# Sum of squares at the head of a projection: seven tiles added on GpSimd, then two ones-products in place of eight

## The chip, the cores and the metric

The kernel runs on one core of a Trainium2 chip. A core has five engines that each take their own queue of instructions in order: TensorE (matrix products, PE in the rows, its weight loads PEld), VectorE (DVE), ScalarE (ACT), GpSimd (POOL) and SyncE (SP, which issues most DMAs). The metric is the device time of one execution in microseconds, and lower is better. Before the change it is 3444.31 us, the median of three runs (3441.16 to 3452.11).

## What is computed

Two blocks stand one behind the other. The first has two layers, each with two attention mixers and an MLP, on 512 tokens of 1024 features. The second has an MLA layer and a GLA layer, each with an MLP, on the same 512 latent tokens and on 256 context tokens. What matters here is the norm ahead of each projection:

```python
def rms_norm(x, g):
    xf = x.astype(jnp.float32)
    y = xf * lax.rsqrt(jnp.mean(xf * xf, axis=-1, keepdims=True) + RMS_EPS)
    return (y * g.astype(jnp.float32)).astype(x.dtype)
...
    x = x + rms_norm(mixed, norm_g[1])
    hf = rms_norm(x, norm_g[2])
    ff = jnp.square(jax.nn.relu(hf @ w_ff1)) @ w_ff2
    return x + rms_norm(ff, norm_g[3])
```

In the second block the norm's output is modulated: `h * (1 + scale) + shift`. So each projection's output goes through a norm, is added to the residual x, and x goes through the next norm, whose output feeds the next projection. All is float32.

## The kernel before

**Layout.** Activations lie feature-major: x is eight tiles (k = 0 to 7) of 128 features on the partitions by the tokens on the free axis. The latent stream L has 512 tokens in two slices `sl` of 256, the context stream C has one slice of 256. A norm's sum runs over features, thus over partitions and over the eight tiles. It is formed on TensorE: a product with a 128 x 128 matrix of ones (`total`, line 280) adds up the partitions and leaves the sum in all of them, in PSUM.

**Projections.** A float32 matrix product is done as three products of rounded operands (`mac3`, lines 211 to 213): an activation has a high and a low part (h, lo), a weight too (wh, wl). Weights come by DMA into a raw tile; ScalarE casts the high part (line 190) and GpSimd, in a few places VectorE, subtracts to get the low one (line 194). The split of weights is the bulk of GpSimd's work.

**The norm at the head.** `sum_sq` squares one tile on ScalarE (line 322) into a scratch tile, the slice of S.y that the residual has just used up or a temporary tile t where there is no y, and makes the product with ones at once, eight products that accumulate in one PSUM tile. `inv_rms` then makes the factor: a Ln on ScalarE (line 146) that reads the PSUM tile, VectorE's copy of the mean into S.acc (line 260), an Exp and three short VectorE steps of a Newton correction. There are two users. `prep_plain` (first block) makes the parts h and lo without the factor, so its matmuls wait for h and lo alone and the factor comes in behind them. `prep_mod` (second block) needs the factor first: sum of eight squares, factor, and then per tile one VectorE, one ScalarE and one VectorE step to h and lo.

**The residual ahead of it.** The steps over k come from `residual`, which makes the previous norm's factor r from S.acc (sum of squares that lines 291 to 299 added up beside the previous projection, some on GpSimd, the rest on VectorE, and one ones-product) and then does for each tile two VectorE instructions, lines 308 and 309:

```python
nc.vector.scalar_tensor_tensor(y, y, gs[:, k:k + 1], r, op0=ALU.mult, op1=ALU.mult)
nc.vector.tensor_tensor(x, x, y, op=ALU.add)
yield k
```

At each yield `sum_sq` squares the new x. Three norms have no residual in front: the two slices of the very first norm, and the context's first norm in the second block; their x comes by DMA. In all there are 19 norms of 256 tokens of this kind: 2 at the start (11 to 38 us), 2 at 493 to 520, 2 at 872 to 902, 2 at 1354 to 1381, the context's first at 1420 to 1447, 2 at 1741 to 1794, 3 at 2111 to 2164, 3 at 2668 to 2731 and 2 at 3040 to 3077.

**The order.** These norms are generators, which the projection in front advances between its groups of matmuls (`chain`, `tick`, `ready`, lines 112 to 132): the norm of slice 0 runs while TensorE still works on slice 1. Each engine's queue is laid out when the program is built, by a scheduler that has its own estimates of durations. On the chip every engine takes its queue strictly in order; an instruction that waits holds up what stands behind it.

Of the kernel before, what the change touches and what calls it, by code (L numbers as in the profile page):

```python
# [14 lines left out]
AF = mybir.ActivationFunctionType  # L15
ALU = mybir.AluOpType
# [6 lines left out]
KT = D // P  # L23
# [27 lines left out]
class Builder:  # L51
# [265 lines left out]
            return S.y[:, k, sl]  # L317
        return self.t(self.tmp, [P, 512], F32, tag="t")[:, :256]

    def sum_sq(self, S, k, sl, ps):  # L320
        q = self.scratch(S, k, sl)
        self.nc.scalar.activation(q, S.x[:, k, sl], AF.Square)
        return self.total(q, ps, k == 0, k == KT - 1)

    def prep_plain(self, S, sl, gs, steps):

        nc = self.nc
        ps = None
        for k in steps:
            h, lo = (p[:, sl] for p in S.ht[k])  # L330
            x, g = S.x[:, k, sl], gs[:, k:k + 1]
            nc.scalar.activation(h, x, AF.Copy, scale=g)  # L332
            nc.vector.scalar_tensor_tensor(lo, x, g, h.bitcast(F32), op0=ALU.mult, op1=ALU.subtract)
            ps = self.sum_sq(S, k, sl, ps)
            yield
        self.inv_rms(ps, D, S.r[:, sl], S.acc[:, sl])

    def prep_mod(self, S, sl, gs, sh, steps):

        nc = self.nc  # L340
        ps = None
        for k in steps:
            ps = self.sum_sq(S, k, sl, ps)
            yield
        r = self.t(self.rp, [P, 256], F32, tag="ry", bufs=6)
        self.inv_rms(ps, D, r, S.acc[:, sl])
        for k in range(KT):
            h, lo = (p[:, sl] for p in S.ht[k])
            t = self.scratch(S, k, sl)
            nc.vector.scalar_tensor_tensor(t, S.x[:, k, sl], gs[:, k:k + 1], r, op0=ALU.mult, op1=ALU.mult)  # L350
            nc.scalar.activation(h, t, AF.Identity, bias=sh[:, k:k + 1])
            nc.vector.scalar_tensor_tensor(lo, t, sh[:, k:k + 1], h.bitcast(F32), op0=ALU.add, op1=ALU.subtract)
            yield
# [1998 lines left out]
```

## Time and profile before

| | |
|---|---|
| time, median of 3 runs | 3444.31 us |
| the profiled execution | 3443.82 us |
| its span, first to last instruction | 3442.1 us |
| mean granted TensorE clock | 0.98 |
| TensorE busy | 3267.2 us, 95% |
| VectorE busy | 2147.2 us, 62% |
| ScalarE busy | 1512.3 us, 44% |
| GpSimd busy | 1174.1 us, 34% |

A row of the timeline has the start, the duration, engine, line, operation, the program's names out<-in, the shape, how many instructions the row merges, and in brackets the idle time of that engine just before, with what ended it. A row that merges several instructions spans from the first one's start to the last one's end, and rows of different lines can lie over each other in time. A float32 product shows as two rows of TensorE. In a window, the granted clock is the share of full speed (1.00 is 2.4 GHz, 0.50 is 1.2 GHz) that TensorE had, as a mean over the stretch. Numbers in brackets behind a busy time are counts of instructions.

### The profile page before, as it was taken

Reading aid. Unit: us, or ns where it says so; the run is one execution under the profiler, and the core shown is the slowest. Engines: PE = TensorE matmul, PEld = TensorE weight load, DVE = VectorE, ACT = ScalarE, POOL = GpSimd, SP = SyncE. Lnnn points to the kernel's source line nnn. Section 1 sums busy time; section 2 is a strip of 40 time slices with the busy share of each in tenths; the row PEclk is TensorE's granted clock in tenths of the full one; section 3 lists DMA queues with packets and bytes.
Section 4 is the critical chain, followed back from the end, with each engine's and each line's share of the span. In section 5 each row is a group of like instructions: output and inputs, shape, how many; then the busy total and the mean of one; then the engine's idle time right before and its main releaser. Section 6 shows DMA issues by size and latency. Waiting matters only on the chain.

```text
span 3442.1 us, 48999 instructions
## 1 busy us (share of the span) xinstructions
PE 3267.2 (95%) x18723; PEld 2826.3 (82%) x18723; DVE 2147.2 (62%) x4036; ACT 1512.3 (44%) x3323; POOL 1174.1 (34%) x688
## 2 busy tenths in 40 slices
PE   8899989999899998999999999999999899989998
PEld 8788778878878877778888878888888888878887
DVE  6855677875875567676577764333334767873445
ACT  5445544232545554422256664422222566653223
POOL 3333334444323333344422332222223222124443
PEclk8999999999999999999999999999999999999999
DMA  5212464553321245465321122122212221123332
GB/s 177 66 61 71 147 196 141 184 166 110 108 68 59 71 147 178 147 197 168 94 69 33 48 88 69 57 67 62 62 62 63 65 63 57 61 77 102 98 98 68
DMA packets 262098, 337.69 MB, mean 98 GB/s; under 512 B 17107, under 2 KB 178110, under 8 KB 261734
## 3 DMA queue, kind: packets, MB, share of 16 engines
q1 hardware_dynamic: 261862, 334.55, 31.0%
q8 instruction: 147, 2.41, 0.3%
q14 instruction: 89, 0.73, 0.1%
HBM read 305.98 MB, written 28.52 MB: 97 GB/s over the span
## 4 chain that ended last, share of the span: by engine, by line
PE 69%; DVE 16%; ACT 7%; issue 4%; DMA 2%; POOL 1%; SPq 0%; DVEq 0%; ACTq 0%; POOLq 0%
PE mm L211 15%; PE mm L213 15%; PE mm L212 15%; PE s L212 4%; PE s L211 4%; PE s L213 4%; PE s L280 2%; ACT wh L190 1%; DMA araw<-in_ada_w_dram 1%; POOL wl L194 1%; PE tp L1065 1%; PE mm L238 1%; PE mm L239 1%; PE mm L240 1%; DVE y L308 1%
## 5 line engine op out<-in xcount | busy, mean ns | idle before, releaser
L194 POOL TENSOR_TENSOR wl<-wraw,wh 128x1024 fp32r<-128x1024 f32 (+2 forms) x424 | 993.3, 2361 | 1750.8 <-ACT wh L190 1703.2
L211 PE MATMUL mm<-h,wh 128*128 128x512 f32 (+1 forms) x1916 | 723.2, 378 | 31.1 <-ACT h L332 9.5
L213 PE MATMUL mm<-h,wh 128*128 128x512 f32 (+1 forms) x1916 | 710.5, 372 | 3.6 <-DVE h L1265 1.6
L212 PE MATMUL mm<-h,wl 128*128 128x512 f32 (+1 forms) x1916 | 711.1, 371 | 0.5 <-DVE wl L194 0.4
L190 ACT CAST wh<-wraw 128x1024 fp32r<-128x1024 f32 (+3 forms) x454 | 428.7, 967 | 534.2 <-issue 366.6
L211 PEld LDWEIGHTS mm<-h,wh 128*128 128x128 f32 x1916 | 367.6, 192 | 94.8 <-ACT h L1264 10.7
L213 PEld LDWEIGHTS mm<-h,wh 128*128 128x128 f32 x1916 | 367.0, 192 | 67.7 <-DVE h L1265 4.8
L212 PEld LDWEIGHTS mm<-h,wl 128*128 128x128 f32 x1916 | 368.0, 192 | 51.9 <-POOL wl L194 0.8
L529 DVE TENSOR_TENSOR t<-t 128x512 f32<-128x512 f32 (+1 forms) x140 | 173.1, 1237 | 255.2 <-ACT hid L525 255.1
L211 PE MATMUL mm<-hid,wh 128*128 128x512 f32 (+1 forms) x848 | 292.5, 345 | 9.8 <-DVE y L541 9.7
L213 PE MATMUL mm<-hid,wh 128*128 128x512 f32 (+1 forms) x848 | 289.9, 342 | 0.0
L212 PE MATMUL mm<-hid,wl 128*128 128x512 f32 (+1 forms) x848 | 289.7, 342 | 0.0
L1381 DVE SCALAR_TENSOR_TENSOR tp<-araw,sc,tp 128x512 f32<-128x512 f32 x280 | 200.7, 751 | 57.6 <-DMA araw<-in_ada_w_dram 56.2
L541 DVE TENSOR_TENSOR y<-y,mm 128x512 f32<-128x512 f32 (+1 forms) x192 | 105.4, 549 | 196.4 <-PE mm L213 196.4
L530 DVE TENSOR_TENSOR hid<-t,hid 128x512 fp32r<-128x512 f32 (+1 forms) x176 | 199.5, 1138 | 29.0 <-ACT t L527 24.3
L213 PE MATMUL s<-hid,wh 128*128 128x512 f32 (+1 forms) x560 | 208.7, 373 | 0.0
L211 PE MATMUL s<-hid,wh 128*128 128x512 f32 (+1 forms) x560 | 208.6, 373 | 0.0
L212 PE MATMUL s<-hid,wl 128*128 128x512 f32 (+1 forms) x560 | 208.4, 372 | 0.0
L525 ACT ACTIVATE hid<-t 128x512 fp32r<-128x512 f32 (+1 forms) x176 | 97.4, 555 | 219.7 <-DVE t L522 144.0
L211 PEld LDWEIGHTS mm<-hid,wh 128*128 128x128 f32 x848 | 159.2, 188 | 34.1 <-DVE y L541 6.8
L213 PEld LDWEIGHTS mm<-hid,wh 128*128 128x128 f32 x848 | 159.2, 188 | 20.9
L212 PEld LDWEIGHTS mm<-hid,wl 128*128 128x128 f32 x848 | 159.2, 188 | 20.8
(683 smaller groups left out, 7362.5 us busy)
## 6 DMA issues: line engine op xcount, KB each, us to landing
wraw<-in_w_ff_dram SPq DMA_DIRECT2D x128, 512.0 KB
wraw<-in_mlp_w_dram SPq DMA_DIRECT2D x128, 512.0 KB
araw<-in_ada_w_dram SPq DMA_DIRECT2D x96, 512.0 KB
wraw<-in_w_in_dram SPq DMA_DIRECT2D x68, 512.0 KB
raw<-in_cmp_w_dram SPq DMA_DIRECT2D x16, 512.0 KB
td<-t SPq DMA_DIRECT2D x32, 256.0 KB
h<-td SPq DMA_DIRECT2D x32, 256.0 KB
wraw<-in_w_out_dram SPq DMA_DIRECT2D x16, 512.0 KB
```

The source lines that it names most:

```text
L190: i = nc.scalar.copy(h[:, x:z], raw[:, x - a:z - a]).ins
L194: e.tensor_tensor(l[:, x:z], raw[:, x - a:z - a], h[:, x:z].bitcast(F32), op=ALU.subtract)
L211: nc.tensor.matmul(ps, wh, mh, start=first, stop=False)
L212: nc.tensor.matmul(ps, wl, mh, start=False, stop=False)
L213: nc.tensor.matmul(ps, wh, ml, start=False, stop=last)
L238: nc.tensor.matmul(ps, h[:, sl], w[0][:, k, :n], start=k == 0, stop=False)
L280: self.nc.tensor.matmul(ps, self.ones, acc, start=first, stop=last)
L525: nc.scalar.activation(h, a, AF.Square)
L529: nc.vector.tensor_tensor(a, a, a, op=ALU.mult)
L530: nc.vector.tensor_tensor(lo, a, h.bitcast(F32), op=ALU.subtract)
L541: nc.vector.tensor_tensor(y, y, ps, op=ALU.add)
L1381: nc.vector.scalar_tensor_tensor(a, raw[:, k], sc, a, op0=ALU.mult, op1=ALU.add)
```

## The change

The square of tile 0 goes to S.acc directly. The squares of tiles 1 to 6 go to the scratch as before, and GpSimd adds each to S.acc (the new line 328). Tile 7's square isn't added: the sum over partitions is now two products, one of S.acc and one of tile 7's square, which accumulate in one PSUM tile. So each of the 19 norms has 2 products where it had 8, and 6 adds on GpSimd. S.acc is free then: the residual in front has read it last in its Newton step. The lines behind move by three.

```diff
--- before.py
+++ after.py
@@ -317,30 +317,33 @@
             return S.y[:, k, sl]
         return self.t(self.tmp, [P, 512], F32, tag="t")[:, :256]
 
-    def sum_sq(self, S, k, sl, ps):
-        q = self.scratch(S, k, sl)
-        self.nc.scalar.activation(q, S.x[:, k, sl], AF.Square)
-        return self.total(q, ps, k == 0, k == KT - 1)
+    def sum_sq(self, S, k, sl):
+
+        nc, acc = self.nc, S.acc[:, sl]
+        q = acc if k == 0 else self.scratch(S, k, sl)
+        nc.scalar.activation(q, S.x[:, k, sl], AF.Square)
+        if k == KT - 1:
+            return self.total(q, self.total(acc, None, True, False), False, True)
+        if k:
+            nc.gpsimd.tensor_tensor(acc, acc, q, op=ALU.add)
 
     def prep_plain(self, S, sl, gs, steps):
 
         nc = self.nc
-        ps = None
         for k in steps:
             h, lo = (p[:, sl] for p in S.ht[k])
             x, g = S.x[:, k, sl], gs[:, k:k + 1]
             nc.scalar.activation(h, x, AF.Copy, scale=g)
             nc.vector.scalar_tensor_tensor(lo, x, g, h.bitcast(F32), op0=ALU.mult, op1=ALU.subtract)
-            ps = self.sum_sq(S, k, sl, ps)
+            ps = self.sum_sq(S, k, sl)
             yield
         self.inv_rms(ps, D, S.r[:, sl], S.acc[:, sl])
 
     def prep_mod(self, S, sl, gs, sh, steps):
 
         nc = self.nc
-        ps = None
         for k in steps:
-            ps = self.sum_sq(S, k, sl, ps)
+            ps = self.sum_sq(S, k, sl)
             yield
         r = self.t(self.rp, [P, 256], F32, tag="ry", bufs=6)
         self.inv_rms(ps, D, r, S.acc[:, sl])
```

Of GpSimd's queue this is the place of the two norms at 493 to 520 us. Names: wl is a weight's low part (line 194), acc_95 is S.acc, t and y are squares. Before:

```order
L194 TENSOR_TENSOR wl_4909<-wraw_4910,wh_4908 128x1024
L194 TENSOR_TENSOR wl_4909<-wraw_4914,wh_4908 128x1024
L299 TENSOR_TENSOR acc_95<-acc_95,t_5060 128x256
L299 TENSOR_TENSOR acc_95<-acc_95,t_5089 128x256
L194 TENSOR_TENSOR wl_5223<-wraw_5224,wh_5222 128x512
L194 TENSOR_TENSOR wl_5223<-wraw_5230,wh_5222 128x512
L299 TENSOR_TENSOR acc_95<-acc_95,t_5141 128x256
L194 TENSOR_TENSOR wl_5249<-wraw_5250,wh_5248 128x512
L194 TENSOR_TENSOR wl_5249<-wraw_5256,wh_5248 128x512
L194 TENSOR_TENSOR wl_5618<-wraw_5619,wh_5617 128x1024
L194 TENSOR_TENSOR wl_5618<-wraw_5623,wh_5617 128x1024
L194 TENSOR_TENSOR wl_5712<-wraw_5713,wh_5711 128x1024
```

Now:

```order
L194 TENSOR_TENSOR wl_5219<-wraw_5220,wh_5218 128x512
L194 TENSOR_TENSOR wl_5219<-wraw_5226,wh_5218 128x512
L299 TENSOR_TENSOR acc_95<-acc_95,t_5137 128x256
L328 TENSOR_TENSOR acc_95<-acc_95,y_4752 128x256 x3
L194 TENSOR_TENSOR wl_5245<-wraw_5246,wh_5244 128x512
L328 TENSOR_TENSOR acc_95<-acc_95,y_4752 128x256 x2
L194 TENSOR_TENSOR wl_5245<-wraw_5252,wh_5244 128x512
L328 TENSOR_TENSOR acc_95<-acc_95,y_4752 128x256 x7
L194 TENSOR_TENSOR wl_5616<-wraw_5617,wh_5615 128x1024
L194 TENSOR_TENSOR wl_5616<-wraw_5621,wh_5615 128x1024
L194 TENSOR_TENSOR wl_5710<-wraw_5711,wh_5709 128x1024
```

The twelve adds of both slices stand among the weight splits, three ahead of the second pair's first split, two between its halves and seven behind.

Of TensorE's queue this is the norm of slice 1 at 2135 us. mm_21058 (now mm_21055) and s_21102 (now s_21099) are tiles of the MLP's first product on slice 0, which needs nothing of this norm; s_20955 (now s_21008) is the norm's sum. Before:

```order
L213 MATMUL mm_21058<-h_20197,wh_21030 128x256
L280 MATMUL s_20955<-y_3748_20259,ones_89 128x256
L211 MATMUL mm_21058<-h_20202,wh_21030 128x256
L212 MATMUL mm_21058<-h_20202,wl_21031 128x256
L213 MATMUL mm_21058<-h_20203,wh_21030 128x256
L280 MATMUL s_20955<-y_3748_20259,ones_89 128x256
L211 MATMUL mm_21058<-h_20021,wh_21030 128x256
L212 MATMUL mm_21058<-h_20021,wl_21031 128x256
L213 MATMUL mm_21058<-h_20022,wh_21030 128x256
L280 MATMUL s_20955<-y_3748_20259,ones_89 128x256 x2
L211 MATMUL s_21102<-h_20148,wh_21030 128x256
```

Now:

```order
L213 MATMUL mm_21055<-h_20194,wh_21027 128x256
L211 MATMUL mm_21055<-h_20199,wh_21027 128x256
L212 MATMUL mm_21055<-h_20199,wl_21028 128x256
L213 MATMUL mm_21055<-h_20200,wh_21027 128x256
L211 MATMUL mm_21055<-h_20018,wh_21027 128x256
L212 MATMUL mm_21055<-h_20018,wl_21028 128x256
L213 MATMUL mm_21055<-h_20019,wh_21027 128x256
L280 MATMUL s_21008<-acc_95,ones_89 128x256
L280 MATMUL s_21008<-y_3745_20256,ones_89 128x256
L211 MATMUL s_21099<-h_20145,wh_21027 128x256
L212 MATMUL s_21099<-h_20145,wl_21028 128x256
```

The products stood two by two between the matmuls of slice 0; now both stand behind the last matmul of the first tile, ahead of the whole next one, and the first of them reads S.acc and so comes behind GpSimd's last add.

## Rows read from the trace of the kernel before

**Rows 1.** The page: busy time by engine (part 1), chain that ended last (part 4).

```profile
PE 3267.2 (95%) x18723; PEld 2826.3 (82%) x18723; DVE 2147.2 (62%) x4036; ACT 1512.3 (44%) x3323; POOL 1174.1 (34%) x688
...
PE 69%; DVE 16%; ACT 7%; issue 4%; DMA 2%; POOL 1%; SPq 0%; DVEq 0%; ACTq 0%; POOLq 0%
PE mm L211 15%; PE mm L213 15%; PE mm L212 15%; PE s L212 4%; PE s L211 4%; PE s L213 4%; PE s L280 2%; ACT wh L190 1%; DMA araw<-in_ada_w_dram 1%; POOL wl L194 1%; PE tp L1065 1%; PE mm L238 1%; PE mm L239 1%; PE mm L240 1%; DVE y L308 1%
```

**Rows 2.** Windows: length, then busy us of PE, PEld, DVE, ACT, POOL, clock, DMA.

```profile
10.00:40.00 30.00, 29.05 (x190) 26.13 (x191) 17.92 (x41) 19.92 (x50) 5.65 (x4) 1.00 0.76 236
490.00:522.00 32.00, 26.97 (x170) 25.04 (x171) 30.45 (x74) 20.12 (x51) 3.73 (x2) 0.89 0.26 83
...
870.00:903.00 33.00, 26.60 (x179) 23.65 (x179) 31.48 (x75) 20.99 (x53) 10.12 (x10) 1.00 0.34 100
...
1420.00:1447.00 27.00, 26.12 (x117) 20.36 (x116) 13.91 (x19) 12.98 (x25) 6.06 (x4) 1.00 0.70 237
...
1774.00:1794.00 20.00, 18.11 (x125) 17.25 (x123) 13.90 (x42) 8.90 (x26) 0.00 (x0) 0.91 0.16 53
...
2131.00:2144.00 13.00, 9.66 (x44) 8.54 (x45) 11.20 (x24) 5.41 (x14) 2.63 (x2) 0.74 0.25 68
...
2701.00:2732.00 31.00, 27.78 (x194) 25.30 (x195) 27.57 (x67) 16.89 (x42) 2.42 (x1) 1.00 0.27 88
3038.00:3054.00 16.00, 10.62 (x53) 9.14 (x52) 14.31 (x24) 7.48 (x18) 7.39 (x5) 0.79 0.23 66
...
514.00:518.00 4.00, 4.00 (x32) 3.85 (x30) 4.00 (x12) 3.13 (x9) 0.00 (x0) 1.00 0.00 0
```

**Rows 3.** Line 280: duration ns min/median/max by operands, and its engine's idle time before.

```profile
L280 PE MATMUL s<-y,ones x256: 377/379/797, 494.2 to 3077.0; 128*128 128x256 f32 x128
...
L280 PE MATMUL s<-t,ones x48: 377/379/634, 12.0 to 1445.0; 128*128 128x256 f32 x48
...
  ACT y L322: 35.5, 32
```

**Rows 4.** Timeline, TensorE: start us, us, what, idle before; four products on end.

```profile
3075.49 1.89 PE L280 MATMUL s<-y,ones 128*128 128x256 f32 x8
```

**Rows 5.** Line 299, the add of squares, on VectorE and on GpSimd: ns min/median/max.

```profile
L299 DVE TENSOR_TENSOR acc<-acc,sq x34: 409/425/2491, 854.1 to 3433.6; 128x256 f32<-128x256 f32 x34
...
L299 POOL TENSOR_TENSOR acc<-acc,sq x24: 726/750/1132, 867.0 to 3431.1; 128x256 f32<-128x256 f32 x24
```

**Rows 6.** Timeline of VectorE and GpSimd in three residual loops and one tail.

```profile
854.10 2.49 DVE L299 TENSOR_TENSOR acc<-acc,sq 128x256 f32<-128x256 f32 x1 [0.48 <-ACT sq L298]
...
874.30 0.62 DVE L308 SCALAR_TENSOR_TENSOR y<-y,g,ry 128x256 f32<-128x256 f32 x1
...
2114.69 0.87 DVE L308 SCALAR_TENSOR_TENSOR y<-y,mod,ry 128x256 f32<-128x256 f32 x2
...
2115.48 0.75 DVE L309 TENSOR_TENSOR x<-x,y 128x256 f32<-128x256 f32 x2
...
2668.86 1.07 POOL L299 TENSOR_TENSOR acc<-acc,sq 128x256 f32<-128x256 f32 x1 [2.27 <-ACT sq L298]
...
2669.26 1.34 DVE L308 SCALAR_TENSOR_TENSOR y<-y,mod,ry 128x256 f32<-128x256 f32 x2
...
2670.53 1.28 DVE L309 TENSOR_TENSOR x<-x,y 128x256 f32<-128x256 f32 x2
```

**Rows 7.** Timeline of ScalarE at the end of the run at 2109.

```profile
2115.93 0.75 ACT L322 ACTIVATE y<-x 128x256 f32<-128x256 f32 x2 [0.71 <-DVE x L309]
...
2117.57 0.47 ACT L146 ACTIVATE ry<-s,eps 128x256 f32<-128x256 f32 x1 [0.21 <-PE s L280]
```

**Rows 8.** Timeline of TensorE and ScalarE in the run at 2135.

```profile
2135.20 1.22 PE L280 MATMUL s<-y,ones 128*128 128x256 f32 x2 [3.22 <-ACT y L322]
...
2139.78 1.44 ACT L322 ACTIVATE y<-x 128x256 f32<-128x256 f32 x4
...
2143.52 0.47 ACT L146 ACTIVATE ry<-s,eps 128x256 f32<-128x256 f32 x1 [2.30 <-PE s L280]
```

## The prediction

> **What bounds the kernel now.** I read the page first, then the windows of the places where a norm's squares are added up, then single rows there. The page says that TensorE is busy 95% of the span, that the chain which ended last runs 69% through TensorE and 16% through VectorE, and that 2% of that chain are ones-products of line 280 [rows 1]. Taken alone this promises up to 2%, some 69 us. But the 19 norms at the head of a projection ("runs" from here on: one run is one norm of 256 tokens) lie at the joints between projections, which aren't average places, so I took windows there [rows 2]. Three kinds show. Where a run has no residual ahead of it (the two at 10 to 40 us, the context one at 1420 to 1447) TensorE is busy 29.05 of 30 and 26.12 of 27 us and VectorE has 12 and 13 us free: TensorE sets the pace. At 1774 to 1794 it is the same, 18.11 of 20. At the joints with a residual loop in front it is VectorE: 30.45 of 32 us at 490, 31.48 of 33 at 870, 14.31 of 16 at 3038, while TensorE has 5 to 6 us free in each. The joint at 2701 stands between, 27.57 against 27.78 of 31. One row speaks against calling the 490 joint VectorE's alone: from 514 to 518 TensorE is busy 4.00 of 4.00 us [rows 2], so its gaps lie in the first half.
>
> **What goes: 114 products.** A run has 8 products now and 2 then; 19 x 6 = 114. In the trace a product is two rows of TensorE, 256 + 48 rows for 152 products [rows 3]. Four products in a row, eight rows, span 1.89 us and a single row 0.38 us [rows 4], so rows start (1.89 - 0.38) / 7 = 0.216 us apart and a product costs 0.43 us at full clock. 114 x 0.43 = 49 us of TensorE: the most that the work itself can give. The products on a residual's square are also what TensorE waits for: 35.5 us in 32 waits for line 322 [rows 3]. Those waits don't go with the products; the next thing TensorE needs is late for the same reason.
>
> **What comes: 114 adds on GpSimd.** The nearest row is the add of line 299, the same operation on the same shape: 0.75 us on GpSimd, 0.43 on VectorE [rows 5]. GpSimd has the room (34% busy [rows 1]) and takes a square every 1.5 us or so, so the 0.75 us count in two other ways.
>
> First, what the add does to VectorE. A residual loop is pairs of lines 308 and 309, without a gap. Two instructions of line 308 span 0.87 us and two of line 309 span 0.75 us with GpSimd silent; with one GpSimd add beside them 1.34 and 1.28 [rows 6]. So one add costs VectorE 0.47 to 0.53 us. In the loop at 874 a single line 308 takes 0.62 us, against about 0.44 for one of the pair: 0.2 us [rows 6]. A VectorE add of 256 columns under a long GpSimd instruction took 2.49 us [rows 6], so the two exclude each other for as long as GpSimd works on that piece. I take 0.5 us per add in a gapless loop; the bounds are 0 (VectorE idle there) and 0.53. The Trainium skill, page "GPSIMD Engine Reference", section "Key points", says that GpSimd shares its SBUF interfaces with VectorE, with contention when the VectorE instruction has two SBUF inputs; both instructions of the loop have. The trace agrees in kind. A reader who let the rule stand for full exclusion would price an add at its whole 0.75 us, and the adds of the residual loops, 16 x 5, at 60 us instead of 40; the rows above have 0.5.
>
> Second, the tail. At the 2109 joint the last two squares end at 2116.68 and the norm's Ln begins at 2117.57 [rows 7]: 0.89 us. In the changed kernel the sixth add can begin when square 6, the first of the two, is done (2115.93 + 0.41 = 2116.34), ends 0.75 us later at 2117.09, two products follow (0.86) and 0.2 us to the Ln: 2118.15, so 0.6 us later. Five adds lie inside the loop, so a run that VectorE sets costs 5 x 0.5 + 0.6 = 3.1 us.
>
> **What moves.** The two products stand together and TensorE, which takes its queue in order, now waits there for GpSimd's last add; behind them are matmuls that need neither. At the 2135 run the first product stands now between matmuls and ten of them come before the last pair; then all products stand behind the 25 matmuls of one group, and 71 ready ones behind the products. Now the last squares end at 2141.22 and the Ln comes at 2143.52 [rows 8], 2.3 us of TensorE's backlog, against 0.75 + 0.86 + 0.2 = 1.8 then: 0.5 us back on the chain. The ten matmuls that fall behind cost 10 x 0.12 = 1.2 us of TensorE (32 rows in 4.00 us at 514 [rows 2]). GpSimd's weight splits (line 194) at the 490 joint stand in between the adds; each add is waited for by no one but the next add and the product, and a split waits at most a loop step of 1.5 us. ScalarE's squares keep their place and length.
>
> **The sum**, against the profiled run's own time of 3443.8 us (span 3442.1 and 1.7 outside; 0.5 below the median):
> - The three runs without a residual: 18 x 0.43 = 7.7 us at most; TensorE is 97% busy there but the tail grows, I take -6.
> - 1774 to 1794: 6 x 0.43 at a granted clock of 0.91 [rows 2]: -2.8.
> - The three joints of two runs each in the first block (490, 870 and its twin of 490 in the next layer). VectorE gets 10 adds, 5 us; TensorE loses 11 products ahead of the last tile, 4.7 us. Ends: +5 if VectorE sets the end, -4.7 if TensorE does. VectorE is gapless all through, TensorE only in the second half, so I stand nearer to the first: +2.5 each, +7.5. No tail here, since the factor is only needed behind the matmuls.
> - 2109 to 2165, three runs: the first +2 of its 3.1 (TensorE has other work until then), the second 3.1 - 0.5, rounded to +3 for the matmuls behind it, the context one 0. +5.
> - 2701, two runs: between -5.2 (12 x 0.43) and +6.2; +2.
> - 3038: +3. The run at 1741: between 0 and 3.1, +1. The run at 2668 and the one at 3068: between -2.6 (its products) and +3.1, taken as 0.
> - The clock. At 2135 TensorE had waited 3.22 us [rows 8] and the granted clock of that window is 0.74, at 3038 it is 0.79 [rows 2]. Now mostly products run at the lower level (1.2 of 2.4 GHz), and their time is hidden by the loop; then the wait is longer and it is ready matmuls that run slow behind it. +2 and +1.
>
> -6 - 2.8 + 7.5 + 5 + 2 + 3 + 1 + 3 = +12.7, so 3456.5 us.
>
> **Rivals.** *TensorE sets the end at the shared joints too*: then the 490-type joints give 3 x -4.7 = -14.1, 2701 -5.2, 3068 -2.6, with -7.7 and -2.8 in the clear places: -32.4. The 1738, 2109, 2135 and 3038 runs still cost some 8: -24, 3420 us. For it: the gapless stretch at 514, and the 2% of the chain. Against: 30.45 of 32.
> *They cancel*: the adds fall where VectorE reads PSUM or idles, at 0.2 us instead of 0.5. Then the first block's joints give 0, 2701 0, and 2109 +2, the clock +1: -8.8 + 2 + 3 + 1 + 1 = -2, 3442 us.
> *Each run pays in full* (the slower end): 16 runs x 3.1 = 50, less 8.8, and 3 us for the clock: +44, 3488 us. It decides where TensorE's next matmul needs the last tile, so nothing of the products is given back. Against it: TensorE's stretch at 514.
> *The change doesn't do what it says* can be left out: the built order has the 114 adds and lacks the products.
>
> **How the numbers follow.** A measurement of this kernel can tell about 0.3%, 10.3 us, from no change: faster lies under 3434.0, slower above 3454.6. My forecast is just beyond that. I give the forecast and what lies above it 0.53 (0.08 of it for full payment), the cancelling case with what lies around it 0.27, the TensorE case 0.20. Range 3430 to 3482: the low end reaches halfway from cancelling to the TensorE case, the high end nearly to full payment.
>
> **What would show it.** Right: line 308 and 309 get longer by 0.5 us per add beside the new line 328; the sum of both lines' busy time grows by 30 to 42 us; the Ln of the 2117 joint begins about 3 us later after its loop's start; TensorE waits some 8 us or more ahead of the pair at 2135. The windows of 10 to 40 and 1420 to 1447 get shorter by 2 us a run. Wrong: TensorE's gaps stay as they are and the 490-type joints end 3 to 5 us earlier; then TensorE's work was the bound and VectorE's longer loop was covered. If line 308 stays at 0.44 us beside the adds, the price itself is wrong.

## The result, and the profile after

The changed kernel takes 3480.55 us (median of 4 runs, 3478.60 to 3481.03) against 3442.82 for the kernel before: 1.0104 times as long, 95% interval 1.0092 to 1.0116. That is 38 us slower. The direction was forecast, the time lies in the range (3430 to 3482) but at its very end; the forecast was 3456.5.

The page of the changed kernel, its span and busy times:

```profile
span 3479.3 us, 48742 instructions
...
PE 3247.7 (93%) x18495; PEld 2808.1 (81%) x18495; DVE 2199.2 (63%) x4036; ACT 1510.3 (43%) x3323; POOL 1270.3 (37%) x802
```

Against [rows 1], TensorE is busy 20 us less (3247.7 for 3267.2), VectorE 52 us more (2199.2 for 2147.2) and GpSimd 96 us more. The 49 us of products didn't all leave TensorE's busy time: the mean granted clock fell from 0.980 to 0.968, and counted in windows of half a microsecond TensorE is busy at the lower of its two levels for 172 us, 119 before. At half speed these 53 us hold some 26 us of extra time.

Where the time was lost can be read by laying the two traces beside each other. I took instructions of VectorE, ScalarE and TensorE that both kernels have in the same number and compared the starts of the first, the second and so on; the median difference behind a place, less that ahead of it, is what the place cost. Between the places the difference stands nearly still.

| place (us before) | forecast | measured |
|---|---|---|
| start to 470, two norms without a residual | -4 | +2.7 |
| 490, two norms | +2.5 | +6.6 |
| 870, two norms | +2.5 | +3.9 |
| 1354, two norms | +2.5 | +5.4 |
| 1420, the context's first norm | -2 | -3.6 |
| 1741 to 1794, two norms | -1.8 | -1.1 |
| 2109 to 2165, three norms | +7 | +11.8 |
| 2668 to 2731, three norms | +2 | +3.8 |
| 3038 to 3079, two norms | +4 | +7.6 |
| everything else | 0 | +0.2 |
| sum | +12.7 | +37.3 |

The windows of some of these places, columns as in [rows 2]:

```profile
10.00:42.00 32.00, 28.14 (x176) 25.16 (x174) 21.18 (x39) 19.69 (x49) 14.22 (x15) 0.89 0.70 221
...
493.00:531.00 38.00, 27.03 (x147) 24.85 (x148) 35.62 (x74) 19.43 (x49) 12.97 (x14) 0.73 0.22 70
...
879.00:916.00 37.00, 25.69 (x164) 22.84 (x162) 36.19 (x73) 20.12 (x50) 19.41 (x23) 0.86 0.25 74
...
2145.00:2168.00 23.00, 9.85 (x53) 8.86 (x53) 21.09 (x39) 10.25 (x26) 11.18 (x9) 0.70 0.30 92
...
3067.00:3091.00 24.00, 10.09 (x50) 8.44 (x48) 21.57 (x32) 10.49 (x22) 15.54 (x13) 0.68 0.16 45
```

The 32 us from 490 of [rows 2] are 38 here, with TensorE busy for the same 27 us and VectorE for 35.6 in place of 30.5. The granted clock there is 0.73 for 0.89, in the windows from 2145 and 3067 it is 0.70 and 0.68 for 0.74 and 0.79. VectorE fills nearly the whole of each but the first.

What VectorE does longer, as groups of its instructions by line (count, then busy us and mean ns); first the kernel before:

```profile
L309 DVE TENSOR_TENSOR x<-x,y 128x256 f32<-128x256 f32 x136 | 62.1, 481 | 0.1
...
L308 DVE SCALAR_TENSOR_TENSOR y<-y,mod,ry 128x256 f32<-128x256 f32 x72 | 39.3, 582 | 0.2
...
L308 DVE SCALAR_TENSOR_TENSOR y<-y,g,ry 128x256 f32<-128x256 f32 x64 | 31.4, 507 | 0.2
...
L333 DVE SCALAR_TENSOR_TENSOR h<-x,g,h 128x256 fp32r<-128x256 f32 x64 | 34.5, 545 | 2.8 <-ACT h L332 2.7
```

and the changed one, where line 333 has become 337:

```profile
L309 DVE TENSOR_TENSOR x<-x,y 128x256 f32<-128x256 f32 x136 | 73.1, 561 | 0.2
...
L308 DVE SCALAR_TENSOR_TENSOR y<-y,mod,ry 128x256 f32<-128x256 f32 x72 | 53.2, 774 | 0.2
...
L308 DVE SCALAR_TENSOR_TENSOR y<-y,g,ry 128x256 f32<-128x256 f32 x64 | 38.7, 626 | 0.1
...
L337 DVE SCALAR_TENSOR_TENSOR h<-x,g,h 128x256 fp32r<-128x256 f32 x64 | 44.3, 706 | 2.4 <-ACT h L336 2.4
```

Lines 308 and 309 together went from 132.8 to 165.0 us, 32 us more; 30 to 42 were forecast. Line 337, the low part in the first block's norms, took another 10, which the prediction had not counted.

The norm of slice 1 that ran at 2135 before shows it in ten rows of the timeline (start, duration, engine):

```profile
2154.35 2.35 DVE L308 SCALAR_TENSOR_TENSOR y<-y,mod,ry 128x256 f32<-128x256 f32 x2
...
2156.37 3.49 POOL L328 TENSOR_TENSOR acc<-acc,y 128x256 f32<-128x256 f32 x4
...
2156.62 1.80 DVE L309 TENSOR_TENSOR x<-x,y 128x256 f32<-128x256 f32 x2
...
2158.34 1.80 DVE L308 SCALAR_TENSOR_TENSOR y<-y,mod,ry 128x256 f32<-128x256 f32 x2
...
2160.52 0.75 ACT L324 ACTIVATE y<-x 128x256 f32<-128x256 f32 x2 [1.65 <-DVE x L309]
...
2161.07 0.92 POOL L328 TENSOR_TENSOR acc<-acc,y 128x256 f32<-128x256 f32 x1 [1.21 <-ACT y L324]
...
2162.05 1.22 PE L280 MATMUL s<-acc,ones 128*128 128x256 f32 x2 [10.55 <-POOL acc L328]
...
2164.16 0.47 ACT L146 ACTIVATE ry<-s,eps 128x256 f32<-128x256 f32 x1 [2.90 <-PE s L280]
...
2164.35 0.41 PE L213 MATMUL s<-h,wh 128*128 128x256 f32 x1
...
2164.57 0.41 PE L211 MATMUL s<-h,wh 128*128 128x256 f32 x1
```

Pairs of line 308 that took 0.87 us [rows 6] take 2.35 beside a weight split and an add, and 1.80 beside adds alone, line 309 likewise 1.80 for 0.75. GpSimd's last add starts at 2161.07, after the square before it, and TensorE has by then waited 10.55 us in front of the first product, as the order foretold; "8 us or more" was forecast. Behind the pair its matmuls start 0.22 us apart (2164.35, 2164.57), which is the lower of the two levels, 1.2 GHz (granted clock 0.50 from 2162 to 2166, behind the wait); at full clock they start 0.12 apart.

In all TensorE waits 65 us for GpSimd's adds in front of products (idle us, times, of the instructions of line 280), where it waited 35.5 us for squares [rows 3]:

```profile
  POOL acc L328: 55.6, 23
  POOL accc L328: 9.2, 4
```

### The profile page after: what moved, and what is told of

Same layout as the page of the kernel before. It is cut to its first block, busy times and chain, and to the rows that moved or that the text cites. A ratio compares the mean times of both kernels' runs of the same rounds, so it can differ in the third digit from the quotient of the medians.

```text
span 3479.3 us, 48742 instructions
## 1 busy us (share of the span) xinstructions
PE 3247.7 (93%) x18495; PEld 2808.1 (81%) x18495; DVE 2199.2 (63%) x4036; ACT 1510.3 (43%) x3323; POOL 1270.3 (37%) x802
## 5 line engine op out<-in xcount | busy, mean ns | idle before, releaser
L211 PEld LDWEIGHTS mm<-h,wh 128*128 128x128 f32 x1916 | 374.3, 195 | 116.9 <-ACT h L336 14.3
L213 PEld LDWEIGHTS mm<-h,wh 128*128 128x128 f32 x1916 | 372.6, 195 | 68.3 <-DVE h L1268 4.8
L211 PE MATMUL mm<-hid,wh 128*128 128x512 f32 (+1 forms) x848 | 293.1, 346 | 15.9 <-DVE y L544 15.8
L533 DVE TENSOR_TENSOR hid<-t,hid 128x512 fp32r<-128x512 f32 (+1 forms) x176 | 206.6, 1179 | 23.5 <-ACT t L530 18.8
```

Source lines behind the costliest of these rows:

```text
L211: nc.tensor.matmul(ps, wh, mh, start=first, stop=False)
L213: nc.tensor.matmul(ps, wh, ml, start=False, stop=last)
L533: nc.vector.tensor_tensor(lo, a, h.bitcast(F32), op=ALU.subtract)
```

## The experiments

Three explanations were set against each other. **A**: the adds cost VectorE its time, and the later sum and the clock behind the longer waits cost the rest. **B**: GpSimd's adds are the whole of it. **C**: only the place of the two products in TensorE's queue matters. Times are differences to the median of the kernel before, from runs on the same chip. For every run the scheduler lays out all queues anew, so a place can move by 2 to 3 us though nothing in it was changed (at 1741 to 1794 the run "Only the norms without a residual", which leaves these norms as they were, is 2 us faster).

**Adds on VectorE.**

```diff
-            nc.gpsimd.tensor_tensor(acc, acc, q, op=ALU.add)
+            nc.vector.tensor_tensor(acc, acc, q, op=ALU.add)
```

> The changed kernel with the 114 adds on VectorE instead of GpSimd. In the changed kernel lines 308 and 309 together got 32 us longer beside the adds. Theory A (the adds cost VectorE its time, and the wait for the last add plus the clock behind it cost the rest): an add costs VectorE 0.42 us in its own queue instead of about 0.4 us of exclusion, so the loops stay as long; the last add comes a little earlier (0.42 for 0.75 us): +25 to +37 us against before. Theory B (GpSimd itself is the trouble, its slow add and its exclusion of VectorE): under +10 us. Theory C (only where the two products stand matters): +37 us.

Measured: 3464.44 us, ratio 1.0061 (1.0044 to 1.0078), +21 us. Less than A said and more than B. The same sums cost 17 us less on VectorE than on GpSimd, but the larger part of the loss stays. An add in VectorE's own queue takes 0.42 us there (the median); on GpSimd an add made VectorE's lines 308, 309 and 337 longer by 0.37 us on average, and came later besides. The Trainium skill, page "GPSIMD Engine Reference", section "Engine selection", names VectorE for an add of two tiles, and GpSimd as about two times slower; the rows agree, with 0.43 us against 0.75 [rows 5], and the two times point the same way.

**The adds beside eight products.**

```diff
-        q = self.scratch(S, k, sl)
+        q = S.acc[:, sl] if k == 0 else self.scratch(S, k, sl)
...
+        if 0 < k < KT - 1:
+            nc.gpsimd.tensor_tensor(acc, acc, q, op=ALU.add)
```

> The kernel before with all eight products kept, and the 114 adds on GpSimd made beside them, their sum used by nobody. It measures what GpSimd's adds do to VectorE without moving a product. Theory A: the loops of lines 308 and 309 get about 30 us longer in sum as in the changed kernel, of which half reaches the end: +12 to +22 us. Theory B (GpSimd's adds are the whole trouble): +30 to +40. Theory C (only where the products stand matters): within 4 us of before.

Measured: 3484.77 us, ratio 1.0120 (1.0105 to 1.0135), +41 us. That is just above B's span, and far from A's and C's. But its trace has a wait of its own: GpSimd's first add overwrites S.acc and so waits for product 0, and the weight splits stand behind it. Who waited for line 280 (us, times):

```profile
  POOL acc L326: 49.0, 7
  POOL accc L326: 16.7, 3
```

So the run was not clean, and was made again without that wait:

**The adds apart.**

```diff
+        if 0 < k < KT - 1:
+            self.nc.gpsimd.tensor_tensor(S.acc[:, sl], q, q, op=ALU.add)
         return self.total(q, ps, k == 0, k == KT - 1)
```

> The kernel before, all products as they were, and on GpSimd 114 instructions acc = q + q on the six middle squares of each norm, read by nobody and waiting for no product (in the run with the adds beside the products the first add of a norm waited for a product, up to 66 us of GpSimd's time in all, and weight splits stood behind it). So this has the exclusion of VectorE alone. If exclusion is the price: VectorE's busy time up by some 42 us and the time by +30 to +42. If the waits of GpSimd's queue made that run slow: under +15.

Measured: 3472.14 us, ratio 1.0080 (1.0065 to 1.0095), +28 us, VectorE busy 30 us more. The forecast for exclusion was +30 to +42 and 42 us of VectorE; both came out smaller, but well above the 15. So the adds alone, with every product where it was and no product waiting for an add, cost 28 us (22 to 33). The adds also stand among GpSimd's weight splits; that is not the price, for TensorE waits for GpSimd's low parts 1.0 us in all, as in the kernel before, and ScalarE 361 us for 370. VectorE's groups in this kernel:

```profile
L309 DVE TENSOR_TENSOR x<-x,y 128x256 f32<-128x256 f32 x136 | 72.4, 555 | 0.1
...
L308 DVE SCALAR_TENSOR_TENSOR y<-y,mod,ry 128x256 f32<-128x256 f32 x72 | 47.8, 699 | 0.2
...
L308 DVE SCALAR_TENSOR_TENSOR y<-y,g,ry 128x256 f32<-128x256 f32 x64 | 38.2, 613 | 0.2
...
L335 DVE SCALAR_TENSOR_TENSOR h<-x,g,h 128x256 fp32r<-128x256 f32 x64 | 39.8, 628 | 2.7 <-ACT h L334 2.4
```

Together they are 31 us longer than before, against 42 in the changed kernel; line 308 in the second block (47.8 for 53.2) and the low part, here line 335 (39.8 for 44.3), make the difference. The stand-in q + q is a milder add: it takes 82 us of GpSimd in all, the real adds 96.

**Two products without adds.**

```diff
-        nc.scalar.activation(q, S.x[:, k, sl], AF.Square)
+        nc.scalar.activation(q, S.x[:, k, sl], AF.Square, scale=2.0)
...
-        if k:
-            nc.gpsimd.tensor_tensor(acc, acc, q, op=ALU.add)
```

> The changed kernel without the adds: the sum has the squares of tiles 0 and 7 alone, each doubled before the square (scale 2 in the activation), so six of eight tiles are left out of the norm and the output is not the reference's. Two products per norm at the end of each run, as in the changed kernel, but no add to wait for and none beside VectorE. Theory A: the loops are as short as before; the wait in one piece stays, +0 to +15 us. Theory B: the products' 49 us of TensorE come back in part: -10 to -30. Theory C: +30 to +37.

Measured: 3419.96 us, ratio 0.9931 (0.9916 to 0.9946), -23.5 us. This rules out C, missed A's +0 to +15, and lies in B's span: the products are worth 23.5 us of their 49 when nothing is added for them. The waits in front of products shrink to some 20 us, from 65 in the changed kernel:

```profile
  ACT y L324: 10.8, 11
  ACT acc L324: 9.1, 9
```

**Adds that no product waits for.**

```diff
-            nc.gpsimd.tensor_tensor(acc, acc, q, op=ALU.add)
+            nc.gpsimd.tensor_tensor(acc, q, q, op=ALU.add)
```

(with the scale of 2 as in the kernel without adds, and the first square in a scratch tile)

> The changed kernel with the two products at the end of each norm, but of the squares of tiles 0 and 7 alone (scale 2; six tiles are left out of the norm, the output is not the reference's), and the 114 GpSimd instructions beside it as acc = q + q, which no product waits for. Against the run without adds (-23.5) it has GpSimd's exclusion of VectorE, against the changed kernel (+37) it lacks the wait for the last add. If the exclusion is all: +19 (-23.5 + 42). If the wait for the last add matters: below +30, and the rest up to +37 is the wait's. If neither adds up: about +37.

Measured: 3459.26 us, ratio 1.0044 (1.0029 to 1.0059), +15 us. So the adds cost 38.5 us here (from -23.5 to +15) when no product needs them, 10 more than beside eight products; and the changed kernel, in which a product needs them, is another 23 us slower (from +15 to +38). Not all of the 23 is the wait: lines 308, 309 and 339 (the low part here) are 33 us longer than before in this run, 9 less than the 42 of the changed kernel, since the stand-in adds are milder here too (81 us for 96). In front of products TensorE waits for squares alone (us, times):

```profile
  ACT y L324: 40.9, 25
```

**Three adds per norm.**

```diff
-        if k == KT - 1:
-            return self.total(q, self.total(acc, None, True, False), False, True)
-        if k:
+        if 0 < k < 4:
             nc.gpsimd.tensor_tensor(acc, acc, q, op=ALU.add)
+        if k == 4:
+            ps = self.total(acc, None, True, False)
+        if k > 3:
+            return self.total(q, ps, False, k == KT - 1)
```

> The changed kernel with only the squares of tiles 1 to 3 added on GpSimd (57 adds in all); five products per norm: of the sum as soon as tile 4's square is there, and of tiles 4 to 7 one by one. No product waits for a late add, and 57 products go. If cost goes by adds: 57 x 0.37 = +21, less 57/114 of the 23.5 that the missing products gave = -12: +9. If the last add's wait is what makes the changed kernel slow: -5 to +3.

Measured: 3475.27 us, ratio 1.0093 (1.0078 to 1.0108), +31 us: a miss for both expectations. Half the adds cost nearly as much. The wait did not go, it moved to the middle of the norm; TensorE's idle time in front of line 280 (us, times):

```profile
  POOL acc L326: 51.3, 22
```

The scheduler lays the product of the sum where it believes the third add done, and the add is later than that. VectorE's busy time rose by 26 us, so the 57 adds cost it as much each as the 114. Why half the adds cost nearly as much as all is not settled further than that.

**The pair later in TensorE's queue.**

```diff
+        for _ in range(2):
+            yield
+        ps = self.total(q, self.total(S.acc[:, sl], None, True, False), False, True)
```

(ahead of `inv_rms`, in place of the pair in `sum_sq`)

> The changed kernel with the pair of products given out two steps of the projection later, so that the scheduler lays it 24 to 47 matmuls further back in TensorE's queue (at the 2135 norm 47 matmuls that need nothing of the norm now stand ahead of the pair). Adds, squares and their places stay. In the changed kernel TensorE waits 10.55 us for the last add in front of the pair there, 65 us in all such places. If the wait in front of ready matmuls is a large part of the loss: 5 to 15 us less than the changed kernel (+22 to +32 against before). If VectorE's longer loops alone set the end: +35 to +40, and the wait only changes its name.

Measured: 3477.28 us, ratio 1.0099 (1.0082 to 1.0115), +35 us. The wait in front of products halves (35 us for 65) and the time hardly moves; the interval takes in the changed kernel's 1.0104. So the matmuls held up behind the pair were at most a small part of the price. At the 2135 norm the 10.55 us are gone, and TensorE now waits for a weight's low part, which VectorE makes behind its longer loop:

```profile
2151.64 2.35 DVE L194 TENSOR_TENSOR wl<-wraw,wh 128x512 fp32r<-128x512 f32 x2
...
2152.90 0.58 PE L212 MATMUL mm<-h,wl 128*128 128x256 f32 x1 [4.35 <-DVE wl L194]
```

**The products as idle work.**

```diff
             nc.gpsimd.tensor_tensor(acc, acc, q, op=ALU.add)
+            S.extra = self.total(q, None if k == 1 else S.extra, k == 1, k == KT - 2)
```

> The changed kernel with six more products per norm, of the squares of tiles 1 to 6, into a PSUM tile that nobody reads: TensorE gets the 114 products back as idle work between the adds, 49 us at full clock, and is not left waiting in one piece. In the changed kernel TensorE is busy at half clock for 172 us against 119 before, 53 us more, which costs up to 26 us. If the clock behind the waits is a large part: half-clock busy time near 120 to 140 us and the time not above the changed kernel, +25 to +37, in spite of 49 us more work. If not: +45 to +60.

Measured: 3486.82 us, ratio 1.0128 (1.0111 to 1.0145), +44 us, 7 more than the changed kernel for 49 us more of TensorE work. TensorE was busy at the lower clock for 142 us, against 172 in the changed kernel and 119 before. The time is above the +25 to +37 that stood for the clock and just under the +45 for the other case, so neither case is met. The run changes two things at once, the work and the clock, and so gives no price for the clock. The wait in front of line 280 is no shorter than in the changed kernel, only in more pieces, and mostly for the squares again (us, times):

```profile
  ACT y L324: 63.7, 69
```

**Only the norms without a residual.**

```diff
-        q = self.scratch(S, k, sl)
+        q = S.acc[:, sl] if S.y is None and k == 0 else self.scratch(S, k, sl)
...
+        if S.y is None:
+            acc = S.acc[:, sl]
+            if k == KT - 1:
+                return self.total(q, self.total(acc, None, True, False), False, True)
+            if k:
+                self.nc.gpsimd.tensor_tensor(acc, acc, q, op=ALU.add)
+            return None
         return self.total(q, ps, k == 0, k == KT - 1)
```

> The change in the three norms alone that have no residual in front (the two at the start and the context's first), the kernel before elsewhere. The prediction put these at -6 us. From the offsets between the traces of before and after the start lost 2 to 3 us and the context's norm gained 3.6: -2 to 0.

Measured: 3440.37 us, ratio 0.9989 (0.9979 to 0.9999), -4 us. The sign of that term was right for the three together, with an interval from -7 to 0; the places show +2.6 for the start and -4.4 for the context.

**One-pass products.** Here the products stay eight and cost less, and nothing moves to another engine.

```diff
-        q = self.scratch(S, k, sl)
+        q = self.t(self.tmp, [P, 512], F32R, tag="t")[:, :256]
         self.nc.scalar.activation(q, S.x[:, k, sl], AF.Square)
-        return self.total(q, ps, k == 0, k == KT - 1)
+        if ps is None:
+            ps = self.ps(pool=self.sp, tag="s")[:, :q.shape[-1]]
+        self.nc.tensor.matmul(ps, self.onesq, q, start=k == 0, stop=k == KT - 1)
+        return ps
```

> The kernel before with eight products per norm where they stood, but each a single-pass fp32r product of a rounded square (0.12 us in place of 0.43), scratch in a temporary tile: 152 x 0.31 = 47 us less TensorE work, no adds, no wait moved. If TensorE's work in these places set the end, -25 to -47 us. By theory A (VectorE sets it at the joints with a residual loop): -6 to -16 us, from the three norms without a residual, the one at 1776 and the tails.

Measured, with the matrix of ones (`onesq`) made as fp32r: 3432.56 us, ratio 0.9964 (0.9953 to 0.9976), -11 us, in A's span. Then with another scratch in the second block:

```diff
-            ps = self.sum_sq(S, k, sl, ps)
+            ps = self.sum_sq(S, k, sl, ps, S.ht[k][1][:, sl])
```

> The kernel before with eight single-pass fp32r products per norm (as in the one-pass run, -11 us), but the rounded squares of the second block's norms go to the low-part tile that the norm fills later, not to the four rotating temporary tiles that the MLP's squares use too. If the shared tiles held the squares back in the one-pass run: -13 to -23 us. If not: -8 to -13, as there.

Measured: 3423.40 us, ratio 0.9944 (0.9931 to 0.9958), -20 us. This beats both kernels. Its busy line, and its products (ns min/median/max), one row each where the float32 product has two:

```profile
PE 3231.3 (94%) x18571; PEld 2795.7 (82%) x18571; DVE 2143.6 (63%) x4037; ACT 1509.4 (44%) x3323; POOL 1179.6 (34%) x687
...
L326 PE MATMUL s<-t,ones x64: 274/283/582, 11.9 to 1374.0; 128*128 128x256 f32 x64
...
L326 PE MATMUL s<-h,ones x64: 274/384/582, 1730.3 to 3058.3; 128*128 128x256 f32 x64
...
L326 PE MATMUL s<-hc,ones x24: 278/286/387, 1412.8 to 2713.4; 128*128 128x256 f32 x24
```

TensorE is 36 us less busy than before and VectorE 4 us; most of what the run without adds won is there, with all eight squares in the sum.

## Why the prediction had the sign and a third of the size

The sign came from the right mechanism: GpSimd's adds lengthen VectorE's loops, and that outweighs the products. Of the three explanations A is nearest, the adds on VectorE and then the late sum, but it missed the 23.5 us that the products give back. The adds alone, with no product moved, cost 28 us. The price of an add was about right too. From the first square of a norm to the end of its last, the 16 norms with a residual take 163.6 us in all before, 209.1 after: 2.8 us more each. The prediction had 5 x 0.5 = 2.5 for the loop. Without the adds (two products only) the 16 loops take 168.0 us, with the adds apart 194.5, with the adds on VectorE 198.7.

What is missing can be placed by laying three more traces beside the kernel before, as in the table above. Each column is one profiled execution, and differences of 2 to 3 us say little.

| place (us before) | forecast | two products, no adds | adds apart, eight products | two products, adds not waited for | changed kernel |
|---|---|---|---|---|---|
| start to 470 | -4 | -1.0 | +1.7 | +2.4 | +2.7 |
| 490, 870 and 1354 | +7.5 | -11.9 | +14.7 | +5.9 | +15.9 |
| 1420 | -2 | -4.2 | -0.5 | -4.0 | -3.6 |
| 1741 to 1794 | -1.8 | -3.8 | +4.0 | -2.2 | -1.1 |
| 2109 to 2165 | +7 | -0.8 | +3.9 | +4.3 | +11.8 |
| 2668 to 2731 | +2 | -3.8 | +5.4 | +2.1 | +3.8 |
| 3038 to 3079 | +4 | +2.2 | +1.7 | +5.3 | +7.6 |

**The cover held in the main.** For the three joints of the first block the prediction set +5 each if VectorE sets the end against -4.7 if TensorE does, and took +2.5. Taken by itself, the measured +6.6, +3.9 and +5.4 look like VectorE's end, with nothing given back. The runs say otherwise: with the products gone and no adds these joints come 12 us earlier, some 4 each, so TensorE's products did count there, as the row at 514 had suggested; with the adds alone they come 15 us later; with both, and no product waiting for an add, 6 us later, where 7.5 was forecast. (The stand-in adds of that run are milder, by 9 us of VectorE in the whole kernel, so with real adds it could be a few us more.) The whole kernel is then 15 us slower, near the forecast of 12.7. The rival "each run pays in full" (3488 us, given 0.08) lies nearest to the measured time, but its condition, that nothing of the products is given back, is not what the runs show; that it is near is luck.

What failed are these terms:

- **The sum's way through GpSimd: "No tail here, since the factor is only needed behind the matmuls", and 0.6 us for a tail elsewhere.** From the run whose products wait for no add to the changed kernel it is 23 us more, 10 of them at the three joints where the tail was put at nothing and 7.5 at 2109 to 2165. The 0.6 us came from a single add in a free queue. At the 2109 norm the time from the last square to the Ln grew from 0.89 us to 2.70, by 1.8; in that run it is 0.79. From the norm's first square the Ln came 4.3 us later than before, where about 3 was forecast. Over the 16 norms this time is 31.4 us in the changed kernel and 22.0 there, 9 us; 6 more are longer loops (209.1 against 202.7), where VectorE's lines are longer beside the real adds; the rest is not assigned. Behind the matmuls the factor is what empties their PSUM tiles. At the 490 joint, VectorE's step that reads a finished tile (line 525, with r) waits for the Newton step of line 289, itself stretched to 0.94 us, and TensorE for line 525:

```profile
517.48 0.94 DVE L289 SCALAR_TENSOR_TENSOR r<-ry,r 128x256 f32<-128x256 f32 x1
...
519.21 0.41 DVE L525 SCALAR_TENSOR_TENSOR t<-mm,r 128x256 f32<-128x256 f32 x1
...
519.67 0.58 PE L211 MATMUL mm<-h,wh 128*128 128x256 f32 x1 [3.77 <-DVE t L525]
```

  TensorE stands for 3.77 us. In the kernel before its waits at this joint lay in the first half, and from 510 to 522 there was none; in the run whose products wait for no add its longest wait from 503 to 533 is 1.49 us. That the matmuls behind the pair pay for the late sum, as the prediction put it at 2135, is at most a small part: with the pair moved back, the wait halves and some 3 us come back.
- **The start, -4 forecast and +2.7 measured.** The prediction counted nothing for the adds, since VectorE had 12 us free there. But the adds and line 337 stand in two chains at the same time:

```profile
14.40 1.62 POOL L328 TENSOR_TENSOR acc<-acc,t 128x256 f32<-128x256 f32 x2 [1.79 <-ACT t L324]
...
14.69 1.61 DVE L337 SCALAR_TENSOR_TENSOR h<-x,g,h 128x256 fp32r<-128x256 f32 x2 [0.22 <-ACT h L336]
```

  Five of line 337 take 4.25 us beside five adds in 4.26, where one took 0.48 and the next came 0.7 later. This explains about 1 us: at 60 us the changed kernel is 0.9 us late, and it falls back further near 65 and 100 us, behind both norms. The first one-pass run, which has no adds, is 2 us late by 140 us as well, and the run with the pair later, which has all of them, only 0.2. So what made the start slower stays open. The gain forecast there is not seen either: with two products and no adds it is 1.0 us of the 4.
- **The clock, +3.** It can't be priced by itself. TensorE is busy 53 us more at the lower level; the idle products took 30 of them away and the kernel got slower by 7, with 49 us of work more.

The steps that held: 0.43 us for a product and 49 us in all as the most that can come back (23.5 did where nothing was added); the slowing of VectorE by GpSimd, with the lines and the size that were named; the 10.55 us in front of the pair; the context's norm.

## What to carry to other kernels

An add that moves from TensorE to GpSimd was paid for by VectorE here: count the VectorE instructions with two SBUF operands that run beside it. Then ask who waits for the last add, and follow what the late result holds up (here the factor, and with it PSUM tiles); that was the largest part of the error. Where two engines are both nearly full, each one's work can count: here fewer products and longer loops both moved the same joints. The product that was too dear was better made cheaper where it stood, by one pass in place of two, than moved.

## What the runs showed of the hardware

The slowing of GpSimd and VectorE is mutual: an add with a median of 0.75 us [rows 5] takes 0.85 (4.26 for five) beside line 337, which takes 0.85 for 0.48 itself. The Trainium skill, page "GPSIMD Engine Reference", section "Key points", has the shared SBUF interfaces; by full exclusion an add would have cost VectorE its 0.75 us, and the sum of lines 308, 309 and 337 shows 42 us for 114 adds, 0.37 each on average, over adds that met these lines and adds that did not.

The mean granted clock was lower in most kernels that took products away: 0.968 in the changed kernel, 0.976 without the adds, 0.975 in the first one-pass run (medians), where the kernel before has 0.978 to 0.982 in its runs. In the second one-pass run it is 0.978, which is no clear difference. Of the 49 us of products the kernel without adds is 40 us less busy.
